# A decoder layer whose instructions are issued by a written list: another list, the same instructions

## The chip, the cores and the metric

The kernel runs on one core of one Trainium2 chip. The core has a matrix engine (PE, which reads its stationary operand through weight loads, PEld), a vector engine (DVE), a scalar engine (ACT), a GpSimd engine (POOL) and a queue for transfers (SP). Each works through its own instructions in the order in which they were issued, and waits for others through semaphores. The metric is the device time in microseconds (us) of one execution; several executions give a median.

## The reference, cut to what matters

One layer of a decoder on 256 positions and 1024 channels, all in float32. A recurrent branch and an attention branch with 8 heads of 128 read the same normalised input; their outputs are gated, merged and projected; a gated feed-forward part with a short convolution follows.

```python
h = rmsnorm(x, norm1_g[l])
u = jnp.einsum('bsd,de->bse', h, w_in[l])
x_rnn, g_rnn, q, k, v, g_br = jnp.split(u, list(cuts), axis=-1)
...
ya = rg_lru(xa, w_r[l], b_r[l], w_i[l], b_i[l], lru_lambda[l]) * jax.nn.gelu(g_rnn)
...
merged = (gates[:, :, 0] * jnp.einsum('bsc,cd->bsd', ya, w_proj_rnn[l])
          + gates[:, :, 1] * jnp.einsum('bsc,cd->bsd', yb, w_proj_attn[l]))
x = x + jnp.einsum('bsd,de->bse', merged, w_out[l])
h = rmsnorm(x, norm2_g[l])
up = causal_dwconv(jnp.einsum('bsd,df->bsf', h, w_up[l]), ffn_conv_w[l], ffn_conv_b[l])
act = jax.nn.gelu(up) * jnp.einsum('bsd,df->bsf', h, w_gate[l])
x = x + jnp.einsum('bsf,fd->bsd', act, w_down[l])
```

With 256 positions and a block of 256, the block-sparse attention is plain causal attention inside one block.

## The kernel before

**Weights and halves.** The weights come from memory in chunks of 1 MB, numbered in the order of use (4 and 5 are the first two of the recurrent input, 22 is the third of the gate "ga", 25 the last of "v"). A chunk is loaded into a buffer `raw` (three of them). ACT rounds it to a short form `hi` (four buffers) and DVE takes the rest `lo = raw - hi` (three buffers). Each product is then three matmuls: hi by hi, hi by lo, lo by hi. A `raw` buffer is free for the next load when its `lo` is done; a `hi` or `lo` buffer is free when PE has read it. Activations are split the same way (`xgh`, `xgl`; `qTh`, `qTl`; `kTh`, `kTl`; `pth`, `ptl`), mostly in 23 buffers of 1024 columns that go round.

**PE's order.** PE works through units of 24 matmuls of 512 columns per chunk: k0 to k3, rx0 to rx3, rg0 to rg3, ri0, q0, q1, ri1, ga0, ga1, q2, q3, v0, v1, ga2, ga3, v2, v3, gb0 to gb3, and so on, to the projections (pr, pa, wo), the feed-forward part (up, gt, and the blocks qA, qB, qC) and the down projection (acc). Small groups for the attention heads stand between: S of head h (six matmuls into tile `s`), and O (six into `o`). Head 3 comes first, then 2, 1, 0, then 4 to 7; S3 stands in v1, S2, S1 and S0 in ga2, S4 in v2, O3 and O0 in gb0 and gb1.

**The turn of q.** The units q2 and q3 leave the second half of q in two PSUM tiles, `q10` and `q11` (first and second 128 positions). Each tile has two readers: ACT squares it (`sqq`, for the norm), and DVE transposes its 32 by 32 blocks (`qd`). From `qd` the data go to memory and come back transposed (`qm`), and ACT and DVE split them into `qTh1` and `qTl1`, which S4 to S7 read.

**Issue.** The program first records every instruction without issuing it: 1130 of ACT, DVE, POOL and the queues, numbered 0 to 1129 as recorded, and 1899 of PE. Then `Later.issue` (lines 232 to 245) goes through the string `ORDER` (line 114 on): a number or a range issues those instructions, and `+n` the next n of PE.

```python
        for r in order.split():
            if r[0] == "+":
                ops += [next(pe) for _ in range(int(r))]
            else:
                ops += [self.ops[n] for n in range(int(r.split("-")[0]), int(r.split("-")[-1]) + 1)]
```

So PE's own order does not depend on the string. What the string sets is the order of each other engine's queue; which of the buffers a tile gets (`Pool.buffer` takes the one whose last use in the list is oldest); and what waits for what, where two instructions touch one tile. All instructions are issued from line 245, so every row of the profile has L245, and they are told apart by their tiles.

The numbers that matter below:

| number | engine | instruction |
|---|---|---|
| 161, 162, 163 | DVE | the first two scale k (`kr`), the third transposes it (`kd`) |
| 214, 286 | DVE | transpose the recurrent gate, `gr` from `gs` |
| 306, 308 / 309, 310 | DVE | sums of the squares of `q00`, `q01` / their transposes `qd` |
| 338, 341 | DVE | `lo` of chunks 18 and 19 (units q2 and q3) |
| 339 | SP | load of chunk 22 |
| 342, 343 | ACT, DVE | `qTh0`, `qTl0` |
| 344, 346 | ACT | squares `sqq` of `q10`, `q11` |
| 345, 347 | DVE | their sums |
| 348, 349 | DVE | transposes `qd` of `q10`, `q11` |
| 392, 393 | ACT, DVE | `hi`, `lo` of chunk 22 (unit ga2) |
| 411, 412 | ACT, DVE | `qTh1`, `qTl1` |
| 415 | DVE | a 128x2 product for the softmax of head 0 |
| 429 | DVE | `lo` of chunk 25 (unit v3) |
| 433 to 435 | ACT | tanh, exp, square for the second half of the recurrent gates (`tt1`, `rt1`, `a21`) |
| 515, 516 | ACT, DVE | `pth0`, `ptl0`, read by O0 |
| 586 to 589 | DVE | scans of the first half (`it0`) |
| 788 | SP | load of a 0.5 MB piece of the gate weight (`wq011`) |

Of the kernel before, what the change touches and what calls it, by code (L numbers as in the profile page):

```python
# [114 lines left out]
26 0 4 24-25 1 3 30 32 28 27 2 29 31 +2 5 +1 6 +1 7 +1 8 +1 9 +2 10 +1 11-13 +2 33-34 +3 35-36 15 +5 14 +2 37-38 +2
39-40 16 +5 41-42 18 +2 43-48 +2 17 +2 19 +3 49 51 50 52 23 +3 20 69 71 +6 55 72 21 +4 53 +2 59 57 +1 56 54 +4 60 22
+6 63 +3 58 +3 65-66 +1 64 61-62 +3 67-68 +19 76-77 +5 74-75 +2 96 105-106 +4 73 +1 99 +1 102 93 108 78-79 +15 104 +9
80 109 81-84 +11 107 +1 70 224-226 85-89 +1 90-91 +1 142-143 +7 110 +3 111-112 92 94 +3 95 187-188 +6 141 +5 114 113
+5 98 190 97 117-119 227-228 115-116 +5 186 +3 100 191 +2 204 +2 229 +7 203 +2 121 101 103 144 120 122 230 123 +1
# [15 lines left out]
511 +4 479 +1 513-514 501 515-516 485 512 488 502 486 503-504 559 +4 536-537 534 +2 535 +2 528 +5 477 +6 597 526 +6
539 560 +6 529 518 530 519 562 561 +1 547 +1 527 +2 563 +11 540-541 531-532 +2 525 +2 629 +8 574 +3 542 +3 549-550 +1
581 +2 551-552 +8 553 +1 557 +1 548 +11 564-566 568 618 +2 546 +1 594 +1 554 543 556 +1 544 +1 619 558 555 575 579
576-578 567 598 +7 620 545 +3 584 +6 569-571 601 +2 592 617 789 603 602 +5 595 +2 582 605 604 +6 596 +2 607 +2 580 +1
608 615 599 613 655 +12 606 +5 585 621 600 609-610 593 583 +13 616 +6 611-612 622-623 +18 627-628 +13 625-626 630 729
731 +4 730 +11 614 787 632 788 +5 640-641 +1 732 +8 634-635 +1 733-734 638 +4 790 +19 796 798 639 +1 624 644 785 +14  # L140
800 631 +6 646-647 +3 648-650 +6 636 633 663 637 +11 645 +4 654 653 652 651 +3 658 664 +1 786 670 +3 642 +1 656 659
643 +1 657 797 799 +15 662 661 +3 671 801 +11 669 +5 677 +6 660 665-666 +2 667-668 +4 697 +3 678 +9 672-673 +4 676 +6
674-675 +7 698 712 +10 696 +1 679-680 683 682 681 +12 695 702 +1 684-685 +3 713 +12 699 694 700-701 711 +12 716-717
+11 715 +10 686-687 +1 692 748 690 688 703 +2 704 725 724 +1 689 +1 691 706 705 708 710 707 709 714 961 751 765 727 +2
735 693 736-737 +2 738-741 +3 750 +9 742 728 743-745 960 +1 746-747 +5 766 +1 749 +10 726 997 +13 793 775-776 +6 791
+5 774 764 996 +9 719 718 720-722 +4 792 +6 998 +1 820 +1 723 752 755 758 +3 753 822 +1 784 +1 794 +2 759 +5 756 +2
803 802 +11 767 +3 821 823 +13 761-762 754 760 768-770 995 771 +11 826-827 +1 835 +4 773 772 +6 825 +1 795 757 +1
837-838 777 841 839 +3 994 +8 824 862 778 +1 804 +1 842 763 836 840 +13 779 782 999 783 +3 780-781 +3 828 +3 863 +1
866 864 +10 861 +2 877 808 816 875 829 +9 814 865 1005 867 +2 813 843 +3 845 +1 891 811 805 +1 878 1006 844 876 +11
812 810 807 +8 926 892 +10 817 +1 890 +1 806 868 1008 869-870 872-873 871 +10 927 +2 848 851 809 815 818 +7 855 854  # L150
849 852 929-930 846 879-880 +1 925 +4 1007 +11 874 955-956 +1 894 +7 819 893 +1 954 883 928 884 882 881 +17 964 958 +3
886-887 857 962 888-889 959 +2 847 858 856 +5 850 853 +3 957 +7 931 +3 932 +2 968 830 963 1009 833 859-860 +5 885 +20
969 965 1010 +3 1000 1002 +7 831 834 967 832 900 966 +2 917 +2 916 +8 1001 1011 1003 1012 +11 1018 1014-1015 +10 1016
918-919 +1 1013 +10 970 +4 1019 1017 1023 +8 971 +3 1024 993 1004 +1 1027 1025 +10 907 912 +1 1022 1021 +5 903 910 906
901 909 904 +6 905 +1 1028 1026 +1 1030 +8 911 908 +1 895-896 898-899 897 +2 1020 +4 1031 +2 1034 +7 902 913-914 +1
1029 +4 933 936 934 937 935 +6 1032-1033 +1 1039 +4 1035 +2 920 +6 1043 915 +2 1040 +11 1038 +3 938 +2 972 974-976 973
+5 1041-1042 +1 1053 +9 922 +2 1036 1078 1076 +1 921 1054 +10 1037 1044 1052 +3 923 +2 939-940 947 +7 950 944 977 +1
1077 +1 1088 +4 1079 +5 951 +2 1045 948-949 +1 1046 1050 1047 1049 1048 +3 941 +2 1091 +4 1089 945-946 952 +4 989 +6
982 987 986 +1 1055 924 +1 1087 +2 1056-1058 1061 1059 984 +5 1060 +5 1092 942-943 +2 1098 985 978 953 981 +5 1051 +1
1080 +7 988 979 1101 +3 1099 +1 1090 +7 1062 +3 1097 1081 1083-1085 1082 1086 +10 1093-1096 980 983 990-991 +2 1102 +8  # L160
1064 +5 1103 1063 1065-1067 +4 1068-1071 +7 1109 +5 1104 +3 1072-1075 +10 1110 +5 1100 +8 992 1106 1105 1107-1108 +5
1112-1113 +45 1111 +6 1114-1115 +5 1116-1117 +1 1118-1119 +3 1120-1121 +5 1122-1123 +3 1124-1125 +1 1126 +6 1128 1127
1129
"""


# [1174 lines left out]
```

## Time and profile before

| | |
|---|---|
| median of 3 executions | 428.87 us (427.77 to 428.91) |
| the profiled execution, its own time | 429.04 us |
| its span, first to last instruction | 427.3 us |
| matmuls | 1908, busy 418.9 us |
| DVE | 439, busy 359.5 us |
| ACT | 382, busy 305.7 us |
| POOL | 101, busy 52.3 us |
| read from memory | 92.63 MB |

The profile shows one execution. A row of the timeline gives the start, the duration, the engine, the operation and the tiles, and in square brackets the idle time of that engine ahead of it with what ended it. Durations of matmuls are modelled and overlap; what tells PE's pace is the step from one start to the next.

### The profile page before, as it was taken

To read this page: it belongs to the slowest core of one execution; us is meant where nothing else is said; L and a number is where in the kernel's file an instruction comes from. 1 tells how busy PE (TensorE), PEld (TensorE's weight loads), DVE (VectorE), ACT (ScalarE), POOL (GpSimd) and SP (SyncE) were. 2 spreads that over 40 slices of the span, in tenths; PEclk is the share of its full clock that TensorE was granted. 3 is DMA by queue.
4 is the path that set the end of the run, shared out by engine and by line. 5 is a ranking of instruction groups with operands and counts; after the bars stand their busy time and mean duration, and the time that the engine had idled before them with its cause. 6 is when DMAs were issued, how large, how long until landed. Compare 5 with 4: busy or idle time off the path is not lost.

```text
span 427.3 us, 5450 instructions
## 1 busy us (share of the span) xinstructions
PE 418.9 (98%) x1908; PEld 348.4 (82%) x1908; DVE 359.5 (84%) x439; ACT 305.7 (72%) x382; POOL 52.3 (12%) x101
## 2 busy tenths in 40 slices
...
GB/s 219 414 359 200 278 306 254 200 253 356 320 203 308 156 292 236 219 357 259 281 275 269 247 151 366 222 232 307 150 267 287 184 156 239 257 217 322 288 2 98
DMA packets 46108, 106.89 MB, mean 250 GB/s; under 512 B 8448, under 2 KB 22656, under 8 KB 43648
## 3 DMA queue, kind: packets, MB, share of 16 engines
...
q10 hardware_dynamic: 720, 0.53, 0.4%
...
q14 instruction: 13, 0.11, 0.1%
HBM read 92.63 MB, written 13.89 MB: 249 GB/s over the span
## 4 chain that ended last, share of the span: by engine, by line
PE 84%; DVE 7%; issue 3%; ACT 2%; DMA 1%; POOL 1%; SPq 0%; DVEq 0%; ACTq 0%
PE acc L245 14%; PE up L245 13%; PE k L245 5%; PE pr L245 5%; PE gb L245 5%; PE qA L245 5%; PE wo L245 5%; PE pa L245 5%; PE rg L245 5%; PE rx L245 5%; PE qC L245 3%; PE gt L245 3%; PE last L245 3%; PE v L245 2%; DVE lo L245 2%
## 5 line engine op out<-in xcount | busy, mean ns | idle before, releaser
L245 DVE TENSOR_TENSOR lo<-raw,hi 128x2048 fp32r<-128x2048 f32 (+1 forms) x64 | 141.7, 2217 | 19.3 <-ACT hi L245 16.1
L245 ACT CAST hi<-raw 128x2048 fp32r<-128x2048 f32 (+1 forms) x64 | 118.4, 1856 | 26.0 <-DMA raw<-in_wpa 6.8
L245 PE MATMUL up<-hi,h2l 128*128 128x512 f32 x80 | 31.1, 389 | 0.0
L245 PE MATMUL up<-hi,h2h 128*128 128x512 f32 x80 | 31.1, 389 | 0.0
L245 PE MATMUL up<-lo,h2h 128*128 128x512 f32 x80 | 31.1, 389 | 0.0
L245 PE MATMUL acc<-lo,fah 128*128 128x512 f32 x78 | 30.4, 390 | 0.0
L245 PE MATMUL acc<-hi,fah 128*128 128x512 f32 x78 | 30.4, 390 | 0.0
L245 PE MATMUL acc<-hi,fal 128*128 128x512 f32 x78 | 30.4, 389 | 0.0
L245 POOL TENSOR_TENSOR rsq<-rsq 128x8 f32<-128x8 f32 x32 | 21.0, 658 | 36.4 <-DVE rsq L245 34.3
L245 ACT ACT_TABLE_LOAD x15 | 19.2, 1283 | 1.4 <-PEq L1331 1.2
L245 PEld LDWEIGHTS up<-lo,h2h 128*128 128x128 f32 x80 | 15.0, 188 | 3.1
L245 PEld LDWEIGHTS up<-hi,h2l 128*128 128x128 f32 x80 | 15.0, 188 | 3.1
L245 PEld LDWEIGHTS up<-hi,h2h 128*128 128x128 f32 x80 | 15.0, 188 | 3.1
L245 PEld LDWEIGHTS acc<-hi,fal 128*128 128x128 f32 x78 | 14.6, 188 | 3.1
L245 PEld LDWEIGHTS acc<-hi,fah 128*128 128x128 f32 x78 | 14.6, 188 | 3.1
L245 PEld LDWEIGHTS acc<-lo,fah 128*128 128x128 f32 x78 | 14.6, 188 | 3.1
L245 DVE TENSOR_TENSOR loq<-wq,hiq 128x1024 fp32r<-128x1024 f32 x12 | 14.5, 1216 | 2.4 <-ACT fu L245 1.4
L245 DVE TENSOR_TENSOR lot<-wq,hit 128x1024 fp32r<-128x1024 f32 x12 | 14.4, 1219 | 2.2 <-PE last L245 1.6
L245 ACT ACTIVATE fu<-fupd,pv 128x256 f32<-128x256 f32 x32 | 14.7, 498 | 1.3 <-DVE fal L245 1.3
L245 DVE TENSOR_TENSOR wq<-wq,wq 128x1024 f32<-128x1024 f32 x12 | 14.5, 1219 | 0.2
L245 PE MATMUL ga<-lo,xgh 128*128 128x512 f32 x32 | 12.6, 394 | 1.8 <-DVE lo L245 1.8
L245 ACT CAST hit<-wq 128x1024 fp32r<-128x1024 f32 x12 | 12.3, 1049 | 2.6 <-DVE wq L245 1.7
(302 smaller groups left out, 1177.5 us busy)
## 6 DMA issues: line engine op xcount, KB each, us to landing
raw<-in_win_fm SPq DMA_DIRECT2D x16, 1024.0 KB, 7.3
raw<-in_wdown SPq DMA_DIRECT2D x11, 1024.0 KB, 6.1
raw<-in_wup SPq DMA_DIRECT2D x10, 1024.0 KB, 5.9
raw<-in_win_tm SPq DMA_DIRECT2D x8, 1024.0 KB, 6.0
...
raw<-in_wpr SPq DMA_DIRECT2D x4, 1024.0 KB, 5.8
raw<-in_wpa SPq DMA_DIRECT2D x4, 1024.0 KB, 6.3
...
```

The costliest lines, as they stand in the source:

```text
L245: getattr(engine, name)(*map(real, a), **{n: real(v) for n, v in k.items()})
```

## The change

Only the string `ORDER` differs. It names the same 1130 numbers and the same 1899 matmuls. Of the 423 instructions of DVE 219 stand at another place in DVE's queue, by at most 10 places; of ACT's 351 it is 205, by at most 12; of POOL's 97 it is 31, by at most 11; of the 259 transfers of SP it is 146, by at most 14. The largest shift on SP is 788, which goes ahead by 14. Its author states three rules by which the new list was searched: the readers of one PSUM tile run in the order in which they are issued; steps that depend on one another are chained; and GpSimd's waits are counted.

Cut to the stretch from unit q2 to unit v3 (chunks 18 to 25), with the lines that begin and end inside other stretches left whole:

```diff
-+1 241-242 +6 222 213 +2 211 223 +5 219 +4 282 +1 221 162 +1 243-246 +10 209 327 +1 193-194 271 263-265 275-278 +2 272
...
-303 330 +2 309 305-306 +3 307 +6 319-320 331 +6 321 +3 337 +3 324 +6 326 323 +1 308 362-363 329 +5 364-365 310 313-314
-311-312 +1 325 322 +2 430 338 +1 340 +8 318 +2 336 +5 341 431 440 +1 366-371 +9 328 339 +5 214 217 215 218 +5 441 334
-+1 372 +2 335 355 +2 373-375 443 286 356 +3 360-361 +7 289 354 287-288 442 432 +3 358 +8 376-378 +4 359 +2 216 +7 290
-+1 572-573 589 588 +2 357 +2 342-343 +3 291 +1 348 344-345 433 392 586 +3 349 351-353 350 346 393 +1 347 449 +6 450
-587 452 +3 451 453 +1 454-458 +11 422 434-435 +4 423 +1 391 +7 425 +2 292 402 421 +5 459-463 +7 380 379 381 +1 538 +2
-387 +3 389 +1 426 +11 394-395 436 388 390 +3 424 +5 382-385 +6 386 +2 428 404 +5 403 405-406 480 483 481 484 482 +5
-407 +2 437 396 411 398 +5 408-410 +5 413-416 397 417 +2 429 +8 447 +2 412 399 418 420 401 419 492 427 +1 444 +2 506
...
++3 179 198 180-181 222 +9 211 223 162 +9 282 +1 221 +1 244-247 +10
...
+165 167 317 +10 332-333 315 +5 166 164 +3 330 +2 309 305 +3 310 312 307 +6 319-320 331 308 306 +6 337 321-322 +12 326
+324-325 +1 362 286 363-364 366 329 +5 314 365 367-368 311 313 +3 214 430 338 +9 318 +2 336 +5 323 340-341 431 440-441
++1 369-372 +9 339 289 328 +5 216-217 215 290 218 288 +5 334 +3 335 +2 373-378 443 442 355-356 +3 360-361 432 +7 354
++15 358-359 +9 357 291 287 +1 572-573 589 +4 392 342-343 586 +4 344 433-435 +3 349 348 351 350 352 588 353 393 345-347
++1 449-450 +6 587 451 453 452 +3 454-455 +1 456 +11 422 +4 423 +1 391 +7 425 +2 402 292 421 +5 457-465 +7 379-380 +3
+387 +3 389 381-382 538 +1 426 +11 395 388 436 394 390 +3 424 +5 383-386 +4 403-404 +4 428 396 405 +5 480 482 484 481
+437 483 +5 407 406 408 410 409 +2 411 398 +10 413-414 412 415 397 416-417 +2 429 +8 447 +2 418 506 420 419 492 399 590
...
```

Sorted by engine, the places that the prediction speaks of are these (ranges shortened):

| queue | before | after |
|---|---|---|
| DVE, ahead of unit ga1 and q2 | `lo16`, `kTl0`, 163, 309, 306, `lo17`, 308, ..., 310, 430, 338, 341, 214, 443, 286 | 163, `lo16`, `kTl0`, 309, 310, `lo17`, 308, 306, ..., 286, ..., 214, 430, 338, 341, 443 |
| ACT, ahead of unit ga2 | 572, 342, 344, 433, 392, 346, 422, 434, 435 | 572, 392, 342, 344, 433, 434, 435, 346, 422 |
| DVE, ahead of unit ga2 | 573, 589, 588, 343, 348, 345, 586, 349, 393, 347 | 573, 589, 343, 586, 349, 348, 588, 393, 345, 347 |
| readers of `q10` in the list | 348 (DVE), then 344 (ACT) | 344 (ACT), then 348 (DVE) |
| DVE, ahead of S4 | 413, 414, 415, 429, 412 | 413, 414, 412, 415, 429 |
| SP, among the writes of heads 6 and 7 | 788 after the load of chunk 38 | 788 ahead of the four writes of head 7 |

More of the change, by code (lines that the diff above doesn't have):

```diff
@@ L114 @@
 ORDER = """
[L115 to L119, printed above, removed]
@@ L120 @@
-124-127 +3 145 +3 168 +1 170 205 +10 169 171 174-175 173 189 172 +1 128 +2 129-131 +1 132-133 231 207 +1 146 135 147
-+5 232 148 +4 208 134 136 +1 149-153 +9 177 +1 206 +1 176 199-201 195-196 182 +2 233-234 154 235 155-156 +4 140 192
-138 137 139 +1 157-158 236 159 +2 212 178 +1 183-185 +1 210 +4 220 +1 237-238 160 239-240 +3 197 179 198 202 180-181
-+1 241-242 +6 222 213 +2 211 223 +5 219 +4 282 +1 221 162 +1 243-246 +10 209 327 +1 193-194 271 263-265 275-278 +2 272
-+3 273 266 +1 247 +1 267-268 +1 248-249 +1 283 +7 294-295 285 +2 269 161 270 274 +2 250-254 +2 300 284 +6 302 301 +2
@@ L125 @@
-255-259 +11 297-298 +4 279-280 316 +2 281 +8 299 332 304 +2 296 260-262 +2 317 +10 333 163 315 +5 165 164 166-167 +3
-303 330 +2 309 305-306 +3 307 +6 319-320 331 +6 321 +3 337 +3 324 +6 326 323 +1 308 362-363 329 +5 364-365 310 313-314
-311-312 +1 325 322 +2 430 338 +1 340 +8 318 +2 336 +5 341 431 440 +1 366-371 +9 328 339 +5 214 217 215 218 +5 441 334
-+1 372 +2 335 355 +2 373-375 443 286 356 +3 360-361 +7 289 354 287-288 442 432 +3 358 +8 376-378 +4 359 +2 216 +7 290
-+1 572-573 589 588 +2 357 +2 342-343 +3 291 +1 348 344-345 433 392 586 +3 349 351-353 350 346 393 +1 347 449 +6 450
@@ L130 @@
-587 452 +3 451 453 +1 454-458 +11 422 434-435 +4 423 +1 391 +7 425 +2 292 402 421 +5 459-463 +7 380 379 381 +1 538 +2
-387 +3 389 +1 426 +11 394-395 436 388 390 +3 424 +5 382-385 +6 386 +2 428 404 +5 403 405-406 480 483 481 484 482 +5
-407 +2 437 396 411 398 +5 408-410 +5 413-416 397 417 +2 429 +8 447 +2 412 399 418 420 401 419 492 427 +1 444 +2 506
-508 510 489 496 494-495 507 493 +1 445 +2 475 +16 467 466 400 +2 464-465 590 468-469 438 +8 448 591 +3 476 520 +2 446
-+2 523 522 509 +2 521 524 505 +3 470-471 490-491 472-473 533 +1 478 +5 474 +1 517 +2 293 +5 498 439 487 497 499 +3 500
@@ L135 @@
[L135 to L163, printed above, removed]
+3 24 26 25 28 1 4 30 32 2 0 29 31 +2 5 33-34 +1 6 35 +1 7 37 +1 8 +1 9 +2 10 +1 11-13 +5 36 15 +5 14 +2 38 +2 39-40 16
++5 41-42 18 +2 43-48 +2 17 +2 19 +3 49-52 23 +3 71 20 27 69-70 224 +6 55 72 22 21 +4 53 +2 59 57 +1 56 54 +4 60 +6 63
@@ new lines @@
++3 58 +3 65-66 +1 64 61-62 +3 67-68 +19 76-77 +5 74-75 +2 105 108 96 106 +4 73 +1 99 +1 109 78 93 79-81 +15 104 +9
+82-86 +11 107 +1 225 87-91 142 92 +2 143 +7 110 95 97-98 +3 111-112 94 +3 187-188 +6 141 +5 113-114 +5 101-102 190
+117-120 226-228 121 229 116 115 +5 186 +3 191 100 +2 204 +2 122 +7 203 +2 103 144-146 123-124 +1 125-129 +6 168 +1 170
++10 169 171 205 175 189 174 173 172 +3 130-133 135 134 230-232 +1 207 +1 147 +5 233 148-149 +4 208 136 +1 150-151
+234-235 152-155 +9 177 +1 206 +1 176 199-201 195-196 182-183 +2 156-157 +4 137 192 139-140 138 +1 158-160 236-240 +2
@@ new lines @@
+210 178 +1 197 184 202 185 +2 213 +3 220 +1 241-243 +3 179 198 180-181 222 +9 211 223 162 +9 282 +1 221 +1 244-247 +10
+219 209 327 +1 193-194 263-266 212 267 275-276 +2 271-272 268 273 277-278 +6 248-253 +1 283 +1 285 +6 294 +2 269-270
+161 274 +2 254-255 +2 300 284 +6 302 295 299 297 301 +2 256-262 +4 303 +7 298 +4 279 304 280 316 +2 281 +10 296 +2 163
+165 167 317 +10 332-333 315 +5 166 164 +3 330 +2 309 305 +3 310 312 307 +6 319-320 331 308 306 +6 337 321-322 +12 326
+324-325 +1 362 286 363-364 366 329 +5 314 365 367-368 311 313 +3 214 430 338 +9 318 +2 336 +5 323 340-341 431 440-441
@@ new lines @@
+400-401 520 427 +1 444 +2 493-494 496 489 495 507-508 510 +1 445 +2 438 475 +16 466-467 +2 468-470 490 +8 448 +3 591
+476 +2 446 +2 505 522 509 +2 523-524 521 +3 439 491 487 471-473 533 +1 478 +5 474 +1 517 537 536 +7 497-499 +3 511 293
++3 501 515 513 +1 479 488 516 +1 500 514 502-503 512 485-486 504 +8 535 534 528 +5 477 +6 526 +3 529-530 597 +3
+559-560 539 +6 518-519 562 561 +2 527 +2 563 +11 540 547 541 531 +2 525 +2 629 +8 574 +6 549-550 532 551-552 +1 542
+581 +2 553 548 619 +9 557 544 +12 564-566 543 568 545 618 +2 546 +2 554 556 555 575 577-579 +2 598 558 576 567 569-570
@@ new lines @@
+620 594 +7 617 +3 584 +6 571 601 +2 592 788 603-604 789 605 602 +5 595 +2 582 +6 596 +2 607 +2 580 +1 608 655 599 615
++6 609 +6 606 +5 621 593 585 613 611 600 610 729 583 +13 616 +6 622-623 625 612 +18 627 +13 626 631 630 628 731-732 +4
+730 +11 787 614 632 790 785 +2 640-641 +12 634-635 +1 733 796 734 638 +23 798 639 +1 624 644 +14 800 +6 646 +3 648 647
+649-650 +6 636 633 637 +11 645 +4 651 654 653 652 +3 657 663-664 +1 786 670 +3 642 +1 656 659 643 +1 797 658 799 801
++15 661-662 +3 671 +11 669 +5 677 +6 660 665-666 +2 667-668 +4 697 +3 678 +9 672-673 +4 676 +6 674-675 +7 698 712 +10
@@ new lines @@
+696 +1 679-680 683 682 684 681 685 +12 695 702 +4 713 +12 699-700 694 701 711 +12 716-717 +11 715 +10 686-687 +1 688
+751 692 750 690 703 727 724 +2 704 725 765 +1 689 +1 706 705 691 710 707 709 708 997 714 961 +2 693 735-737 +2 738-742
++12 743-745 +1 728 746-747 +5 766 +11 774 726 +13 775 791 793 749 748 776 +11 998 764 960 +9 719 718 720-722 +4 792 +6
+996 +2 723 752-753 755 758 820 822 759 +4 784 +1 802 794 +9 754 803 761 +11 756 +3 768 821 823 760 +13 767 769 772
+770-771 995 +11 826-827 +5 773 +6 825 +1 795 757 +1 778 835 837 762-763 836 838 +3 994 +8 777 862 841 824 839 +1 804
@@ new lines @@
++1 842 840 +13 779 782 999 +3 781 780 783 845 +6 1005 863 +1 828 866 864 +10 861 +2 877 875 808 829 +9 867 865 +2 843
+813-814 807 891 811 816 805 +5 1006 876 878 844 +11 815 812 810 +8 926 892 +10 817 +1 890 +1 851 868 806 848 809 857
+1008 869 872 870-871 873 +10 927 +2 879 846 929-930 849 818 +7 855 854 852 955 819 880 1007 +1 925 +13 893 +2 874 830
+956 +1 962 964 +8 882 928 881 883-884 833 954 +17 958 +3 886-888 894 889 959 +2 847 853 850 858 856 +8 885 831 957 +7
+931 +5 968 963 965 859 1009 860 +25 969 1010 +10 832 834 966 900 967 +2 917 +2 916 +8 1002 1000 932 1003 1001 1011
@@ new lines @@
+1014 +11 1016 1018 1015 +10 918 +1 1013 +10 970 +3 971 +1 1012 1017 1019 919 1023 +11 1024 993 1004 +1 901 907 1025
++11 1022 1021 +5 909 912 904 1027 906 903 +6 905 +1 1026 1028 +1 910 1030 +9 895 899 898 896-897 +2 1020 +4 1031 +9
+1034 902 913 911 908 933 914 +1 1029 +4 935-936 934 937 +6 1032 1035 1033 +1 1039 +6 920 +6 915 1043 +2 1040 +11 1038
++3 938 +2 972-974 976 975 +5 1041 +1 1053 +9 921 +2 1036 922-923 1076 1078 +1 1054 1042 1044 +10 1037 1052 +5 940 939
+947 950 +7 977 +1 1077 +1 1088 944 +9 951 948 1079 949 +2 1045-1046 1048 1050 1049 +1 1047 +3 941 +2 1091 +4 1089
```

5 lines of the change are left out of this document (added).

## The prediction

> **What bounds the kernel now.** I read the page first.
>
> ```profile
> span 427.3 us, 5450 instructions
> ...
> PE 418.9 (98%) x1908; PEld 348.4 (82%) x1908; DVE 359.5 (84%) x439; ACT 305.7 (72%) x382; POOL 52.3 (12%) x101
> ```
>
> PE is busy for 98% of the span. A new order of the other queues cannot shorten PE's work; it can only take away what PE waits for. So the second view is PE's waits.
>
> ```profile
> PE s L245 <- DVE qTl L245: 2.3, 1, 2.3
> PE ga L245 <- DVE lo L245: 1.8, 1, 1.8
> ```
>
> The columns are total, count and longest. Past the start, PE waits only twice: the third matmul of S4 for `qTl1`, and the second of unit ga2 for `lo` of chunk 22. The third view is PE's timeline at both.
>
> ```profile
> 99.04 0.39 PE L245 MATMUL q<-hi,xgh 128*128 128x512 f32 x1
> 99.27 0.39 PE L245 MATMUL q<-lo,xgh 128*128 128x512 f32 x1
> ...
> 121.50 0.47 PE L245 MATMUL ga<-hi,xgh 128*128 128x512 f32 x1
> 123.80 0.50 PE L245 MATMUL ga<-lo,xgh 128*128 128x512 f32 x1 [1.83 <-DVE lo L245]
> ...
> 139.53 0.28 PE L245 MATMUL s<-kTl,qTh 128*128 128x128 f32 x1
> 142.14 0.33 PE L245 MATMUL s<-kTh,qTl 128*128 128x128 f32 x1 [2.34 <-DVE qTl L245]
> ...
> 143.18 0.39 PE L245 MATMUL v<-hi,xgl 128*128 128x512 f32 x1
> ...
> 144.09 0.63 PE L245 MATMUL v<-hi,xgl 128*128 128x512 f32 x1
> 144.52 0.63 PE L245 MATMUL v<-hi,xgh 128*128 128x512 f32 x1
> ...
> 147.05 0.40 PE L245 MATMUL v<-hi,xgh 128*128 128x512 f32 x1
> ```
>
> From start to start a matmul of 512 columns takes 0.23 us (99.04 to 99.27). The first stop costs 123.80 - 121.50 - 0.23 = 2.07 us. The second costs 142.14 - 139.53, less about 0.1 for a matmul of 128 columns, so 2.5 us. Behind it the step is 0.43 us (144.09 to 144.52): the ten steps from 143.18 to 147.05 take 3.87 us where ten of 0.227 would take 2.27. That is 1.6 us more, at half pace, and the windows below show a granted clock of 0.93 there and 1.00 around. The three terms are 2.07 + 2.5 + 1.6 = 6.17 us.
>
> **What the new order does to the first stop.** The next views are the timelines of ACT and DVE ahead of it.
>
> ```profile
> 116.56 0.69 ACT L245 ACTIVATE sqq<-q,rs 128x512 f32<-128x512 f32 x1 [6.04 <-DVE qd L245]
> 117.27 1.28 ACT L245 ACT_TABLE_LOAD   x1
> 118.56 1.06 ACT L245 ACTIVATE tt<-rt 128x1024 f32<-128x1024 f32 x1
> 119.53 1.89 ACT L245 CAST hi<-raw 128x2048 fp32r<-128x2048 f32 x1
> ...
> 136.60 1.05 ACT L245 ACTIVATE qTh<-qd 128x1024 fp32r<-128x1024 f32 x1
> ```
>
> ```profile
> 112.26 1.22 DVE L245 TENSOR_TENSOR it<-it,tt 128x1024 f32<-128x1024 f32 x1
> 113.51 1.27 DVE L245 TENSOR_TENSOR_SCAN it<-rt,it 128x256 f32<-128x256 f32 x2
> 114.70 1.20 DVE L245 TENSOR_TENSOR qTl<-qd,qTh 128x1024 fp32r<-128x1024 f32 x1
> 115.82 0.71 DVE L245 STREAM_TRANSPOSE qd<-q 128x512 f32<-128x512 f32 x1
> 117.28 0.69 DVE L245 TENSOR_REDUCE sq<-sqq 128x4 f32<-128x512 f32 x1 [0.76 <-ACT sqq L245]
> ...
> 121.45 2.29 DVE L245 TENSOR_TENSOR lo<-raw,hi 128x2048 fp32r<-128x2048 f32 x1 [2.28 <-ACT hi L245]
> ```
>
> ACT stands idle for 6.04 us until DVE has transposed `q10`, though the square does not read `qd`: both read one PSUM tile, and the second reader in the list waits for the first. Behind the square stand a table load (1.28), the tanh (1.06) and only then `hi` of chunk 22; DVE pauses 0.76 + 2.28 = 3.04 us. The new list puts 344 ahead of 348, and 392 ahead of 342, 344 and the tanh. So `hi` starts when the chunk is there.
>
> ```profile
> 100.23 0.49 SPq L245 DMA_DIRECT2D raw<-in_win_fm  x1
> ...
> raw<-in_win_fm SPq DMA_DIRECT2D x16, 1024.0 KB, 7.3
> ```
>
> Its load is issued at 100.23, or at most 2.5 us later if `lo19` slips (next part), and with the group's median of 7.3 us it lands by 110.0. Then `hi` ends at 111.9 and `qTh0` (1.05) at 113.0. DVE's new queue from 113.5 is a scan, `qTl0`, a scan, two transposes, a scan and `lo`: 0.6 + 1.2 + 0.6 + 0.7 + 0.7 + 0.6 + 2.29 = 6.7, so `lo` is done at 120.2. PE wants it at 121.50 + 0.23 = 121.73. The stop goes with 1.5 us to spare, and -2.07 us is the term. The moved transposes now wait for ACT's squares (`q10` at 113.7 at the latest), which come first here.
>
> **The second stop.**
>
> ```profile
> 138.66 2.29 DVE L245 TENSOR_TENSOR lo<-raw,hi 128x2048 fp32r<-128x2048 f32 x1
> 140.87 1.22 DVE L245 TENSOR_TENSOR qTl<-qd,qTh 128x1024 fp32r<-128x1024 f32 x1
> ```
>
> `qTl1` stood behind `lo` of chunk 25 (2.29) and a product of 0.16; now both are behind it. That is 2.45 us earlier, and the 3.04 us that DVE no longer pauses make it 140.87 - 5.49 = 135.4, done at 136.6. PE, 2.07 us ahead, is there at 142.14 - 2.5 - 2.07 = 137.6. One microsecond is to spare. It needs `qTh1` by 135.4, which now ends at 137.65: ACT must come 2.3 us earlier, and the pause that it loses is 6.04. The term is -2.5. `lo25`, which waits 1.2 us longer, is used a unit later.
>
> **The slow matmuls** go with the second stop: the slow pace is there within 2 us of it (142.14 to 144.09), and the first stop, shorter by 0.4 us, left none: the clock is 1.00 in the window around it. The term is -1.6. The Trainium skill (TensorE: Matmul & The Clock Gate, "What's actually happening") has the clock fall to half after at least one idle window of about 3.4 us, so by it a wait of 2.3 us would leave the clock alone. The measured half pace behind 2.34 us of waiting decides here; what the rule would leave is the first rival.
>
> **What the new order costs.** Each place below could give some back.
>
> ```profile
> 83.91 2.29 DVE L245 TENSOR_TENSOR lo<-raw,hi 128x2048 fp32r<-128x2048 f32 x1 [0.58 <-ACT hi L245]
> ...
> 89.90 0.69 DVE L245 TENSOR_REDUCE sq<-sqq 128x4 f32<-128x512 f32 x1 [0.76 <-ACT sqq L245]
> ...
> 95.72 2.28 DVE L245 TENSOR_TENSOR lo<-raw,hi 128x2048 fp32r<-128x2048 f32 x1
> ...
> 102.56 1.24 DVE L245 STREAM_TRANSPOSE gr<-gs 128x1024 f32<-128x1024 f32 x1
> ```
>
> Unit q2: two transposes of `gr`, 1.24 us each, now precede `lo18`, which ended at 98.00 and is wanted at 99.27. That is 2.48 against 1.27, so 1.2 us late. But 163 moves into the pause of 0.58 us, and 310 into that of 0.76: 1.34 us come back, and 0.1 is to spare. Bounds 0 and 1.2; I take 0, since those pauses end on ACT and both moved instructions have their data.
>
> Units v3 to gb3: PE is 6.17 us ahead of its old times; the others must follow.
>
> ```profile
> 119.00:142.00 23.00, 18.98 (x95) 15.63 (x93) 20.11 (x43) 22.24 (x31) 7.42 (x13) 1.00 0.62 217
> 142.00:165.00 23.00, 22.86 (x104) 19.20 (x105) 21.76 (x45) 22.47 (x30) 0.00 (x0) 0.93 0.84 265
> 165.00:183.00 18.00, 18.00 (x96) 15.39 (x95) 17.09 (x31) 17.93 (x26) 0.00 (x0) 1.00 0.70 221
> ```
>
> ```profile
> 159.25 0.56 DVE L245 TENSOR_TENSOR ptl<-pd,pth 128x384 fp32r<-128x384 f32 x1 [0.23 <-ACT pth L245]
> ...
> 162.19 0.28 PE L245 MATMUL o<-ptl,vh 128*128 128x256 f32 x1
> ...
> 192.70 2.29 DVE L245 TENSOR_TENSOR lo<-raw,hi 128x2048 fp32r<-128x2048 f32 x1 [2.16 <-PE pr L245]
> ...
> 204.13 0.39 PE L245 MATMUL pa<-lo,ybh 128*128 128x512 f32 x1
> ```
>
> The busy columns are PE, PEld, DVE, ACT and POOL. DVE (20.11 of 23, 21.76 of 23, 17.09 of 18) and ACT (22.24, 22.47, 17.93) have hardly a pause, so they come forward by what they no longer wait: 3.04 us and up to 6.04. The tightest product is `ptl0`, done at 159.81 and wanted at 162.19: 2.38 to spare. With DVE 3.04 earlier that covers 5.42 of 6.17, so PE could wait 0.75 us at O0; if nothing came forward, 3.8. The writes and the read of `pd0` are issued earlier in the new list. Between 0 and 3.8 I take 0.3, half of the DVE figure, and count it in the forecast. Where the other engines wait for PE itself, they come forward with it.
>
> The queues: 788, moved ahead on SP by 14 transfers, brings 0.5 MB, 2.4 us at the 221 GB/s of that window, ahead of head 7's writes and the load of chunk 34. `lo34` ends at 194.99 and is used at 204.13; 9.1 - 6.2 - 2.4 is still positive, so 0. The buffer that it fills was last read by S7, which PE has then passed, so SP does not stop there. POOL's moved steps interleave two chains that both end before a waiting DVE step; I take 0, with the 0.3 as its bound.
>
> **The sum.** The profiled execution took 429.04 us, 1.74 outside its span. 429.04 - 6.17 + 0.3 = 423.17; the median lies 0.17 under it. The forecast is **423.0 us**, 1.4% faster.
>
> **The rivals.**
> - *The slow pace stays.* If its cause were not the stop (the rule named above), only 4.57 us go: 428.87 - 4.57 = 424.3. For it: a shorter stop left the pace alone. Against: the clock is under 1.00 only in the window that begins with that stop.
> - *Given back at the heads.* DVE and ACT, full, do not follow; O0 waits up to 3.8 us, over 2.3, and half pace follows with 1.6: 423.0 - 0.3 + 5.4 = 428.1 at worst; at 2 us, without the slow pace, 424.7. With the 1.2 us of q2, 425.9.
> - *The stops stay.* If the reader that waits is set by something else than the list, ACT keeps its 6.04 us, `qTh1` holds S4, and little changes: 428.5.
> - *Slower: chunk 22 lands late.* In the new ACT queue `hi22` blocks `qTh0` and the square, and so DVE's `qTl0` and transposes. From the end of `hi22`, `qTh0`, `qTl0`, two scans, two transposes and `lo22` take 1.05 + 1.2 + 1.2 + 1.4 + 2.29 = 7.1 us, so PE stops from a landing at 121.73 - 7.1 - 1.89 = 112.7 on. A landing X later costs X + 1.6 at ga2 and X - 1 + 1.6 at S4. Above X = 2, that is a landing over 12 us after issue, it costs more than 5.9; at X = 4 it is 428.87 - 6.17 + 10.2 = 432.9. The median landing of 7.3 speaks against it.
>
> **How the numbers follow.** Forecast 0.57; slow pace stays 0.05; given back 0.20; stops stay 0.08; slower 0.10. A change of 0.3% (1.3 us) is about the least that a measurement of this kernel tells from none. Faster by more than that is under 427.6: forecast, slow pace and nearly all of "given back", 0.80. Within: the stops that stay and the rest of that, 0.11. Slower: 0.09. The range runs from 422.0 (no wait at O0, and 0.7 of spread) to 427.4 (nearly the worst of "given back") and leaves out the last two cases.
>
> **What would show it.** Right: PE's waits hold neither `ga <- lo` nor `s <- qTl`; no step of 0.43 us after the start; a granted clock of 1.00 throughout; ACT's 6.04 us in front of `sqq` gone; `lo22` ends by 120.5 and `qTl1` by 137. Wrong: a new wait of PE on `q <- lo`, `o <- ptl`, `wo <- ml` or `acc <- fal`, above all one over 2 us with slow steps behind it.

## The result, and the profile after

The changed list takes **423.19 us** in the median of 4 executions (422.61 to 423.42) against 428.74 for the list before (4 executions, 427.77 to 428.91). The ratio is 0.9873, with a 95% interval from 0.9855 to 0.9891: 1.3% faster. The forecast was 423.0. The profiled execution took 422.61 us; that of the kernel before took 429.04, so between the two profiles lie 6.43 us.

The first page lines of the changed kernel, span, busy time and the chain that ended last (its rows have L243, since the string is two lines shorter):

```profile
span 420.8 us, 5449 instructions
...
PE 416.6 (99%) x1908; PEld 347.2 (83%) x1908; DVE 358.5 (85%) x439; ACT 307.5 (73%) x382; POOL 51.1 (12%) x101
...
PE 99%; DVE 0%; issue 0%
```

The busy times of DVE, ACT and POOL are within 2 us of what they were. The chain that ended last is PE almost alone (99%). PE's waits, all of them:

```profile
PE warm L243 <- DVE ones L243: 1.0, 1, 1.0
```

That one is the start. Both rows of before, `ga <- lo` and `s <- qTl`, are gone. PE's timeline at the two places, and at O0, where a new wait was feared:

```profile
121.76 0.39 PE L243 MATMUL ga<-lo,xgh 128*128 128x512 f32 x1
...
137.47 0.27 PE L243 MATMUL s<-kTh,qTl 128*128 128x128 f32 x1
...
155.88 0.28 PE L243 MATMUL o<-ptl,vh 128*128 128x256 f32 x1
```

The first two are the matmuls that waited in the kernel before, the third is the one feared for. The second of ga2 starts at 121.76 instead of 123.80, 2.04 us earlier; the third of S4 at 137.47 instead of 142.14, 4.67 earlier; the second of O0 at 155.88 instead of 162.19, 6.31 earlier. So the gain comes in three steps of 2.04, 2.63 and 1.64 us, and PE keeps it to the end. The windows of the same two stretches as before:

```profile
119.00:142.00 23.00, 23.00 (x117) 19.52 (x116) 22.23 (x52) 20.79 (x31) 7.53 (x13) 1.00 0.75 250
142.00:165.00 23.00, 23.00 (x121) 19.64 (x120) 21.78 (x42) 22.63 (x31) 0.00 (x0) 1.00 0.85 259
```

The columns are those of before: PE is busy for all of both stretches, and the granted clock, third from the end, is 1.00 in both (0.93 in the second before). What made it possible, on ACT and on DVE:

```profile
107.86 1.90 ACT L243 CAST hi<-raw 128x2048 fp32r<-128x2048 f32 x1
...
110.61 0.67 ACT L243 ACTIVATE sqq<-q,rs 128x512 f32<-128x512 f32 x1
```

```profile
114.27 2.26 DVE L243 TENSOR_TENSOR lo<-raw,hi 128x2048 fp32r<-128x2048 f32 x1
...
131.98 1.22 DVE L243 TENSOR_TENSOR qTl<-qd,qTh 128x1024 fp32r<-128x1024 f32 x1
...
151.93 0.56 DVE L243 TENSOR_TENSOR ptl<-pd,pth 128x384 fp32r<-128x384 f32 x1 [0.28 <-ACT pth L243]
```

The square has no bracket now: the 6.04 us ahead of it are gone. `lo22` ends at 114.27 + 2.26 = 116.5 and is read at 121.76; `qTl1` ends at 133.2 and is read at 137.47; `ptl0` ends at 152.5 and is read at 155.88. So PE finds them ready with 5.2, 4.3 and 3.4 us to spare, far more than was worked out (1.5, 1.0 and -0.75).

### The profile page after: what moved, and what is told of

Same layout as the page of the kernel before. It is cut to its first block, busy times and chain, and to the rows that moved or that the text cites. A ratio compares the mean times of both kernels' runs of the same rounds, so it can differ in the third digit from the quotient of the medians.

```text
span 420.8 us, 5449 instructions
## 1 busy us (share of the span) xinstructions
PE 416.6 (99%) x1908; PEld 347.2 (83%) x1908; DVE 358.5 (85%) x439; ACT 307.5 (73%) x382; POOL 51.1 (12%) x101
## 4 chain that ended last, share of the span: by engine, by line
PE 99%; DVE 0%; issue 0%
PE acc L243 14%; PE up L243 13%; PE k L243 5%; PE gb L243 5%; PE pr L243 5%; PE qA L243 5%; PE wo L243 5%; PE ga L243 5%; PE v L243 5%; PE q L243 5%; PE pa L243 5%; PE rg L243 5%; PE rx L243 5%; PE qC L243 3%; PE last L243 3%; PE gt L243 3%
## 5 line engine op out<-in xcount | busy, mean ns | idle before, releaser
L243 DVE TENSOR_TENSOR lo<-raw,hi 128x2048 fp32r<-128x2048 f32 (+1 forms) x64 | 141.7, 2216 | 14.8 <-ACT hi L243 9.4
L243 ACT CAST hi<-raw 128x2048 fp32r<-128x2048 f32 (+1 forms) x64 | 118.7, 1860 | 26.8 <-DMA raw<-in_wpa 7.1
L243 PE MATMUL up<-hi,h2l 128*128 128x512 f32 x80 | 31.1, 389 | 0.0
L243 PE MATMUL up<-hi,h2h 128*128 128x512 f32 x80 | 31.1, 389 | 0.0
L243 PE MATMUL up<-lo,h2h 128*128 128x512 f32 x80 | 31.1, 389 | 0.0
L243 PE MATMUL acc<-lo,fah 128*128 128x512 f32 x78 | 30.4, 389 | 0.0
L243 PE MATMUL acc<-hi,fah 128*128 128x512 f32 x78 | 30.4, 389 | 0.0
L243 PE MATMUL acc<-hi,fal 128*128 128x512 f32 x78 | 30.3, 389 | 0.0
L243 POOL TENSOR_TENSOR rsq<-rsq 128x8 f32<-128x8 f32 x32 | 18.7, 585 | 29.5 <-DVE rsq L243 27.5
L243 DVE TENSOR_TENSOR loq<-wq,hiq 128x1024 fp32r<-128x1024 f32 x12 | 14.4, 1220 | 4.0 <-PE up L243 3.2
L243 PEld LDWEIGHTS up<-hi,h2l 128*128 128x128 f32 x80 | 15.0, 188 | 3.1
L243 PEld LDWEIGHTS up<-hi,h2h 128*128 128x128 f32 x80 | 15.0, 188 | 3.1
L243 PEld LDWEIGHTS up<-lo,h2h 128*128 128x128 f32 x80 | 15.0, 188 | 3.1
L243 PEld LDWEIGHTS acc<-hi,fah 128*128 128x128 f32 x78 | 14.6, 188 | 3.1
L243 PEld LDWEIGHTS acc<-lo,fah 128*128 128x128 f32 x78 | 14.6, 188 | 3.0
L243 PEld LDWEIGHTS acc<-hi,fal 128*128 128x128 f32 x78 | 14.6, 188 | 3.0
L243 DVE TENSOR_TENSOR lot<-wq,hit 128x1024 fp32r<-128x1024 f32 x12 | 14.1, 1221 | 2.4 <-PE acc L243 1.8
L243 ACT CAST hiq<-wq 128x1024 fp32r<-128x1024 f32 x12 | 12.1, 1051 | 4.3 <-PE up L243 3.5
L243 ACT ACTIVATE fu<-fupd,pv 128x256 f32<-128x256 f32 x32 | 14.6, 510 | 0.7 <-DVE fal L243 0.7
L243 DVE TENSOR_TENSOR wq<-wq,wq 128x1024 f32<-128x1024 f32 x12 | 14.6, 1218 | 0.1
L243 POOL TENSOR_SCALAR decw<-decw 128x8 f32<-128x8 f32 x17 | 11.1, 652 | 20.4 <-ACT decw L243 19.1
```

Of the source, the lines that this page charges most:

```text
L243: getattr(engine, name)(*map(real, a), **{n: real(v) for n, v in k.items()})
```

## The experiments

Three questions were put. Which part of the long diff carries the gain? Are the two moves that the prediction named enough, or needed? And is the half pace behind S4 the price of the stop? The diffs show the places of the string at which a kernel differs from the list named.

**The early part alone, the late part alone.** The string was divided at the 294th matmul (unit ri0, 70.6 us). `early_only` has the new list up to there and the old one behind; `late_only` the reverse.

> The new list up to unit ri0 (PE time 70.6 us), the old list from there. Theory E (the early part matters: GpSimd's chain for the norm of k ends 5 us earlier there, and DVE's wait of 2.3 us for it at 57 us is gone): DVE and ACT run about 2.3 us ahead from 70 us on; in the old order behind, lo of chunk 22 then ends at about 121.4 against 121.7 wanted, so the first stop is gone or under 0.3 us; qTl1 ends at 139.8 at the latest against 137.6 wanted, so a second stop of 1 to 2.2 us stays. Time 423.5 to 426.0. Theory L (only the moves next to the stops matter): both stops stay as they were, 428.7 within 0.5.

> The old list up to unit ri0, the new list from there. Theory L, as the prediction worked it out: both stops gone, lo of chunk 22 done by 119 and qTl1 by 136.6, slow pace gone, 422.7 to 423.2. Theory E: without the early part DVE has 2.3 us less to spare; a wait of up to 1.2 us comes back at unit q2 (lo of chunk 18), or a small one at S4, 423.5 to 425.

`early_only`: 426.23 us (424.72 to 427.57, 10 executions), ratio 0.9958 (0.994 to 0.9976). `late_only`: 422.84 us (422.29 to 422.89, 4), ratio 0.9882 (0.9862 to 0.9902), which cannot be told from the full change. The late part alone is enough for the whole gain; the early part alone brings a third of it (0.4%), which is not added to it when both are there. PE's waits in `late_only`, and what is left at S4 in `early_only`:

```profile
PE warm L244 <- DVE ones L244: 1.0, 1, 1.0
PE k L244 <- ACT his L244: 0.2, 1, 0.2
```

```profile
137.31 0.28 PE L245 MATMUL s<-kTl,qTh 128*128 128x128 f32 x1
139.50 0.33 PE L245 MATMUL s<-kTh,qTl 128*128 128x128 f32 x1 [1.92 <-DVE qTl L245]
```

The early part does bring DVE forward, by 2.6 us at `lo22` and `qTl1`, most of it the 2.3 us that DVE waited for `rk` at 57 us, and that removes the first stop by itself: `lo22` ends at 121.1 in `early_only`, PE needs it at 121.72. But it leaves a second stop of 2.1 us (139.50 - 137.31, less 0.1), with steps of 0.43 us behind it in this profile. The median lies 0.2 us above the expected range, in which the half pace was not counted. Where the late part is there too, the early part buys only reserve: in `late_only` `lo22` starts at 116.31 and `qTl1` at 133.82, 2.0 and 1.8 us later than in the full change, and still done 3.3 and 2.6 us before PE needs them.

**One move: the square ahead of the transpose** (`reader_only`, the list before with this):

```diff
-+1 348 344-345 433
++1 344 348 345 433
```

> The old list with one number moved: the square 344 of q10 ahead of the transpose 348 of the same PSUM tile. If the list alone decides which reader waits: ACT's pause of 6.0 us ahead of the square goes, hi of chunk 22 ends at 115.4, DVE no longer pauses and lo ends at 120.7 (wanted 121.7): the first stop gone; DVE comes 3.0 us forward, so qTl1 ends at 139.1 against 137.6 wanted: a second stop of 1.5 us instead of 2.5. With the slow pace gone (it needs a longer stop) 424.0, with the slow pace staying 425.6. If something else sets the reader that waits: 428.7, unchanged, with ACT's pause still there.

424.43 us (424.22 to 424.97, 4), ratio 0.9924 (0.9904 to 0.9944): a single swap, alone, is worth about 60% of what the whole change is worth. The ACT timeline shows the chain that the prediction named:

```profile
110.70 0.66 ACT L245 ACTIVATE sqq<-q,rs 128x512 f32<-128x512 f32 x1
111.38 1.28 ACT L245 ACT_TABLE_LOAD   x1
112.67 1.06 ACT L245 ACTIVATE tt<-rt 128x1024 f32<-128x1024 f32 x1
113.64 1.90 ACT L245 CAST hi<-raw 128x2048 fp32r<-128x2048 f32 x1
118.16 0.69 ACT L245 ACTIVATE sqq<-q,rs 128x512 f32<-128x512 f32 x1 [2.62 <-DVE qd L245]
```

The square starts 5.86 us earlier than before (116.56), and `hi22` 5.89 earlier (119.53). The 2.62 us at the end are the same wait again, for the other tile: 346 still stands behind 349. So the list decides which of two readers of one PSUM tile waits. PE's timeline at S4:

```profile
137.17 0.28 PE L245 MATMUL s<-kTl,qTh 128*128 128x128 f32 x1
138.98 0.33 PE L245 MATMUL s<-kTh,qTl 128*128 128x128 f32 x1 [1.53 <-DVE qTl L245]
```

The second stop is 1.7 us (1.81 less 0.1) instead of 2.5, since DVE came forward by more than PE did; no step of 0.43 us follows it.

**The other cure of the first stop** (`hi22_ahead`, the list before with `hi22` ahead of `qTh0`, the square left where it was):

```diff
-+2 342-343 ... 433 392 586
++2 392 342-343 ... 433 586
```

> The old list with one move: 392 (hi of chunk 22) ahead of 342, so also ahead of the square 344, which still waits for DVE's transpose 348. Theory (the first stop has two causes in series: the square that waits 6.04 us, and hi of chunk 22 that stands behind it): hi22 starts when its chunk is there and ends by 112, lo of chunk 22 no longer pauses 2.28 us for it, and the first stop is 0 to 0.3 us instead of 2.07. The square still waits for the transpose, so ACT and DVE come forward by less than in reader_only, qTl1 still stands behind lo of chunk 25, and S4 stops for 2 to 4 us because PE arrives 2 us sooner. Time 424.5 to 426.5 us, the spread being the half pace behind that stop. Rival (the reader order alone carries the first stop): hi22 early only moves the wait, ga2 still stops for about 2 us and the time stays at 427.5 to 428.9.

426.98 us (425.41 to 428.25, 10), ratio 0.9967 (0.9946 to 0.9989); the median lies 0.5 above the expected range. The ACT timeline:

```profile
109.69 1.92 ACT L245 CAST hi<-raw 128x2048 fp32r<-128x2048 f32 x1
...
116.68 0.69 ACT L245 ACTIVATE sqq<-q,rs 128x512 f32<-128x512 f32 x1 [4.11 <-DVE qd L245]
```

and PE at S4, where the matmul before started at 137.59:

```profile
140.46 0.47 PE L245 MATMUL s<-kTh,qTl 128*128 128x128 f32 x1 [2.60 <-DVE qTl L245]
```

The square starts as late as before, and yet the first stop is gone: `lo22` ran from 119.22 and ended 0.5 us ahead of PE. So the two moves are two cures of one stop. But here ACT keeps its wait, `qTl1` came forward by only 1.7 us (139.19) and PE by 1.9, and the stop at S4 stays: 2.8 us (140.46 - 137.59, less 0.1).

**Two moves** (`three_moves`, which in spite of its name has two: the swap of `reader_only`, and `qTl1` ahead of `lo25`):

```diff
-+1 348 344-345 433 ... +5 413-416 397 ... +2 412 399
++1 344 348 345 433 ... +5 413-414 412 415-416 397 ... +2 399
```

> The old list with two numbers moved: 344 ahead of 348, and qTl1 (412) ahead of 415 and of lo of chunk 25 (429). If the two stops are all that the new list takes away: both gone, lo of chunk 22 at 120.7, qTl1 at 136.6 against 137.6 wanted, 422.7 to 423.2, the time of the whole new list. If the other 600 moved places carry a share of the gain, it stays above 424.

424.61 us (423.81 to 426.42, 6), ratio 0.9929 (0.9908 to 0.995). Not what was expected: both stops are gone, the half pace too, and the time is that of `reader_only`. PE's timeline at O0 has what took it back:

```profile
155.75 0.39 PE L245 MATMUL gb<-hi,xgl 128*128 128x512 f32 x1
156.90 0.39 PE L245 MATMUL o<-pth,vh 128*128 128x256 f32 x1 [0.76 <-ACT pth L245]
157.49 0.39 PE L245 MATMUL o<-ptl,vh 128*128 128x256 f32 x1 [0.21 <-DVE ptl L245]
```

156.90 - 155.75 - 0.23 and 157.49 - 156.90 - 0.11 make 1.4 us. In this list ACT rounds `pth0` at 156.34, behind two exponentials and two copies of v; in the full new list it does so at 151.40, behind one exponential. The rival "given back at the heads" is real, and the rest of the new list is what prevents it. One of the six executions (426.42) has a granted clock of 0.996, which the profiled one does not show.

**`pth0` as well** (`pth0_too`: the two moves, and 515 and 516 moved ahead by a few places):

```diff
-+3 500 ... +1 513-514 501 515-516 485
++3 515 500 ... +1 513 516 514 501 485
```

> The run with two moves (344 ahead of 348, qTl1 ahead of lo of chunk 25) has no stop at ga2 and S4, but PE waits at O0, because ACT comes to pth0 (515) at 156.3 only, behind two exps and two copies of v. This kernel adds two moves: 515 ahead of 500, 516 ahead of 514. If ACT's order is what gives 1.4 us back at O0: pth0 starts when the read of pd0 has landed, about 154.6, ptl0 ends at 155.7, PE wants them at 155.7 and 155.9, so the wait at O0 is under 0.3 us and the time 423.0 to 423.5. If the transfer of pd0 is what is late (its writes and its read are issued 6 us later than in the new list): pth0 stays at 156 and the time near 424.5.

424.79 us (423.53 to 427.4, 10), ratio 0.9925 (0.9901 to 0.9949), so no faster than `three_moves`, and above both expected times. In the profiled execution (423.75 us) the wait at O0 is gone and PE reads `pth0` at 155.87, within 0.11 us of the full list. ACT rounds `pth0` at 153.02 there, so the transfer of `pd0` was not what was late. PE's waits show one further on:

```profile
PE warm L245 <- DVE ones L245: 1.0, 1, 1.0
PE pr L245 <- DVE yal L245: 0.4, 1, 0.4
```

The matmul that waits starts 0.78 us behind the one before it (180.45 to 181.23) instead of 0.23, a loss of 0.55. That profile supports a wait that moves on. The median of all ten lies another microsecond up, and what those executions lose was not seen; two of them (426.87 and 427.40) have a granted clock of 0.995.

**The full list without the two moves** (`undo_both`: the new list with 348 ahead of 344 and 412 behind 429 again):

```diff
-+4 344 ... 349 348 351 ... +10 413-414 412 415 397 ... 429 +8
++4 348 344 ... 349 351 ... +10 413-415 397 ... 429 412 +8
```

> The new list with both moves taken back: 348 ahead of 344 again, and lo of chunk 25 ahead of qTl1. If each of the two moves carries its own term of the prediction, the stops return: 425 to 429. If the new list holds more than is needed (its qTl1 ends 4.3 us before PE wants it, lo of chunk 22 5.2 us before): ACT's square starts about 3 us later than in the new list and qTl1 ends 2.3 to 4.5 us later, at 135.5 to 137.7 against 137.5, so at most 0.3 us of waiting: 422.7 to 423.7.

423.23 us (422.63 to 423.31, 4), ratio 0.9884 (0.9855 to 0.9913): as fast as the full change. PE's timeline at S4 and DVE's ahead of it:

```profile
137.88 0.28 PE L244 MATMUL s<-kTl,qTh 128*128 128x128 f32 x1
137.99 0.27 PE L244 MATMUL s<-kTh,qTl 128*128 128x128 f32 x1
```

```profile
134.25 2.29 DVE L244 TENSOR_TENSOR lo<-raw,hi 128x2048 fp32r<-128x2048 f32 x1
136.46 1.22 DVE L244 TENSOR_TENSOR qTl<-qd,qTh 128x1024 fp32r<-128x1024 f32 x1
```

`qTl1` ends at 137.68, 0.3 us ahead of PE. Neither move is needed once everything else stands as in the new list: `hi22` is ahead of the square there, so that the square's wait for the transpose, which is back (2.81 us), does not hold it up; and the rest brings DVE forward by 4.4 us (140.87 to 136.46).

**The stop put back.** The new list issues `qTl1` five or seven times more in a row (the diff shows seven; the line that asserts the number of instructions is left out):

```diff
-413-414 412
+413-414 412 412 412 412 412 412 412 412
```

> The new list, with qTl1 (412) computed five times more ahead of itself; its value does not change. Each costs DVE 1.15 us, 4.3 us are to spare, so PE stops at S4 for about 1.4 us. If the slow pace needs an idle time of a whole window of about 3.4 us, or one close to the 2.5 us of the old list, no step of 0.43 us follows: 424.2 to 424.8, all executions alike. If any stop of over a microsecond brings it: 425.8 to 426.4.

> The new list, with qTl1 computed seven times more: PE stops at S4 for about 3.7 us. If the length of the stop brings the slow pace, it follows in every execution: 422.9 + 3.7 + 1.6 = 428.2, within 0.5. If the slow pace of the old list came from something other than the stop: 426.6.

`late_by_5`: 425.8 us (425.39 to 426.71, 8), ratio 0.9951 (0.9935 to 0.9967). `late_by_7`: 429.88 us (428.46 to 430.37, 8), ratio 1.0035 (1.0015 to 1.0055). PE's timeline of `late_by_5`, then that of `late_by_7`, where the stop begins at 137.47:

```profile
137.68 0.28 PE L243 MATMUL s<-kTl,qTh 128*128 128x128 f32 x1
139.88 0.33 PE L243 MATMUL s<-kTh,qTl 128*128 128x128 f32 x1 [1.93 <-DVE qTl L243]
...
140.92 0.39 PE L243 MATMUL v<-hi,xgl 128*128 128x512 f32 x1
141.15 0.40 PE L243 MATMUL v<-hi,xgh 128*128 128x512 f32 x1
```

```profile
142.20 0.48 PE L243 MATMUL s<-kTh,qTl 128*128 128x128 f32 x1 [4.45 <-DVE qTl L243]
...
143.22 0.63 PE L243 MATMUL v<-hi,xgh 128*128 128x512 f32 x1
143.65 0.63 PE L243 MATMUL v<-lo,xgh 128*128 128x512 f32 x1
```

Both stops are longer than was expected (2.1 us, which is 139.88 - 137.68 less 0.1, for 1.4; 4.6, which is 4.73 less 0.1, for 3.7). The stop of 2.1 us left the pace at 0.23. So `late_by_5` fell into the range that was expected with the half pace (425.8 to 426.4) without it: the longer stop makes 2.1 of its 2.6 us. The stop of 4.6 us halved the pace at once. The two further copies made the stop 2.5 us longer and the kernel 4.1 us slower (425.8 to 429.88); the 1.6 us above the stop are about what the nine steps of 0.43 us in its profile cost over nine of 0.227, 1.8 us.

**The kernel before, three times more** (unchanged; `before_again_1` to `_3`).

> The kernel before, unchanged, for a second profile. Theory A (the 2.5 us stop at S4 brings the half pace in some executions only): the stop at ga2 is 2.0 to 2.1 and that at S4 2.4 to 2.6 us again; the time is near 427.2 where no steps of 0.43 us follow, and near 428.8 where they do. Theory B (the same stop always brings them, and the two groups of times differ in something else): ten steps of 0.43 us in this profile too, whatever its time.

> As before_again_1, a third profile. Theory A: of the three profiles of this kernel at least one has no steps of 0.43 us and takes about 1.6 us less than one that has them. Theory B: all have them.

> The kernel before once more. Its executions with a granted clock of 0.995 or 0.996 lie in two groups, 426.96 to 427.84 and 428.18 to 429.82. If this one falls in the lower group, theory A (only the start differs from execution to execution) has the first matmul of ga2 1 to 1.6 us earlier than the 121.50 of the first profile, with both stops and the slow pace unchanged; theory B (the stops differ) has it at 121.5 and the stops or the slow pace shorter by that much. If it falls in the upper group it only adds a fourth profile with stops of 2.0 to 2.1 and 2.4 to 2.6 us.

429.84, 427.5 and 427.75 us. The timeline of PE around S4 and the window of that stretch, in `before_again_2`:

```profile
139.61 0.28 PE L245 MATMUL s<-kTl,qTh 128*128 128x128 f32 x1
142.22 0.33 PE L245 MATMUL s<-kTh,qTl 128*128 128x128 f32 x1 [2.33 <-DVE qTl L245]
...
144.20 0.39 PE L245 MATMUL v<-hi,xgh 128*128 128x512 f32 x1
144.43 0.40 PE L245 MATMUL v<-lo,xgh 128*128 128x512 f32 x1
```

```profile
142.00:165.00 23.00, 22.78 (x114) 19.37 (x115) 21.77 (x45) 22.49 (x30) 0.00 (x0) 1.00 0.84 264
```

The same of `before_again_1`:

```profile
140.01 0.28 PE L245 MATMUL s<-kTl,qTh 128*128 128x128 f32 x1
142.62 0.33 PE L245 MATMUL s<-kTh,qTl 128*128 128x128 f32 x1 [2.34 <-DVE qTl L245]
...
144.01 0.63 PE L245 MATMUL v<-hi,xgh 128*128 128x512 f32 x1
144.44 0.63 PE L245 MATMUL v<-lo,xgh 128*128 128x512 f32 x1
```

```profile
142.00:165.00 23.00, 22.38 (x102) 18.77 (x103) 21.77 (x45) 22.48 (x29) 0.00 (x0) 0.93 0.82 262
```

The same stop to 0.01 us, once with the half pace behind it and once without. `before_again_3` has the stop (2.61 from start to start) and no slow step either. So the stop brings the half pace in some executions only. `before_again_3` was to tell why the times of this kernel that come with a clock of 0.995 or 0.996 lie in two groups. Its clock was 1.00, so that stays open.

## Why the prediction was right, and where its steps were not

**The three terms.** The forecast was 423.0 us, the median is 423.19. The terms 2.07, 2.5 and 1.6 us, together 6.17, measured 2.04, 2.63 and 1.64, together 6.31 at O0 and 6.43 in the profiled times. That the stops, and not PE's work, were what a new order could take away is shown by the waits after. That the median agrees to 0.2 us is in part luck: the profiled execution (422.61) is 0.56 us faster than the sum for it (423.17), because the 0.3 us at O0 did not occur and the terms are 0.26 larger; and the median lies 0.58 above that execution, not 0.17 under it.

**The first stop.** The chain transpose, square, table load, tanh, `hi22` is shown by `reader_only`. The prediction told the reader order and the early `hi22` as one cure; they are two, and each is enough (`reader_only`, `hi22_ahead`). The early part of the list is a third (`early_only`).

**The second stop.** `qTl1` ahead of `lo25` was counted as its cure. It is one (`three_moves` has no wait there), but `undo_both` shows that in the full list it is not needed. The prediction's term was right, its cause too narrow: of the 8.9 us by which `qTl1` came earlier (140.87 to 131.98), 2.45 are the swap and the rest is DVE's lead; 4.4 us come without either move (`undo_both`).

**The step that failed: how far DVE and ACT come forward.** The prediction let DVE gain 3.04 us, the two pauses at chunk 22, and put the moved steps of POOL at 0. DVE's wait for POOL at 57 us stood in the profile of before and was not weighed. POOL's timeline in the kernel before, then DVE's:

```profile
51.33 2.25 POOL L245 TENSOR_TENSOR rsq<-rsq 128x8 f32<-128x8 f32 x1 [4.03 <-DVE rsq L245]
53.54 0.20 POOL L245 TENSOR_TENSOR decw<-decw 128x8 f32<-128x8 f32 x1
```

```profile
51.23 2.29 DVE L245 TENSOR_TENSOR lo<-raw,hi 128x2048 fp32r<-128x2048 f32 x1
...
56.99 0.69 DVE L245 TENSOR_TENSOR kr<-kr,rk 128x512 f32<-128x512 f32 x1 [2.27 <-POOL rk L245]
```

The POOL operation of 53.54, of the same kind and size, took 0.20 us; that of 51.33 took 2.25, and ended at 53.58, with DVE's subtraction (53.52). At 57.71 another one takes 2.32 us, beside DVE's next subtraction (57.69 to 59.97). The Trainium skill (SBUF — State Buffer, "Who interferes with whom") says that a DVE instruction with two SBUF inputs contends with a GpSimd instruction that reads SBUF, and that the shared pair of ports is an exclusive lock; these rows agree. Without the 2.05 us that POOL lost there, DVE's pause would, by these rows, have been some 0.2 us. In the new list POOL's chain runs while DVE is not subtracting, and ends at 51.9, 5.1 us earlier than before (56.96):

```profile
51.39 0.21 POOL L243 TENSOR_TENSOR rk<-rsq 128x8 f32<-128x8 f32 x1
51.68 0.20 POOL L243 TENSOR_TENSOR rk<-rk,rs 128x8 f32<-128x8 f32 x1
```

At most 2.05 of these 5.1 us can be the blocked operation. The larger part is the 4.03 us in the brackets above: POOL waited for a small step of DVE (`rsq`, at 51.02), which stood behind another subtraction (47.52 to 49.80) in the old list. In the new one DVE does the three small steps for this norm together (45.05), ahead of its next subtraction (45.52). No run moved these steps alone; `early_only` moves them with the rest of the early part, and has no wait for `rk`. So DVE's pause of 2.27 us falls away, and DVE is ahead from 55 us on (`kr` at 54.59 instead of 56.99). At q2 `lo18`, given 0.1 us to spare, had 3.4 (done at 95.9, wanted at 99.30); in `late_only`, which still has the pause (2.24 us), it had 0.6 (98.8, wanted at 99.44).

A second part was in the prediction's own rows: the pauses of 0.58 and 0.76 us ahead of q2, into which 163 and 310 move, were counted at q2 and not behind it. In `late_only`, where both are gone, the scan that was taken to start at 113.5 starts at 112.20. With these 1.3 us, and the 2.0 and 1.8 of the early part, the 1.5 and 1.0 us to spare at the two stops become 4.8 and 4.1; measured were 5.2 and 4.3. The step made the forecast's reserves too small, not its time wrong: `late_only` is as fast without the early part's 2 us.

**The 0.3 us at O0** did not occur. It was bounded by letting `ptl0` come forward with DVE's 3.04 us; it came 7.3 us forward (159.25 to 151.93), and 5.6 in `late_only`, where PE still had 1.8 us to spare at O0. That the danger was rightly placed is shown by `three_moves`, which pays 1.4 us there.

**The slow matmuls.** The term of 1.6 us is right for the profile that it was read from, and taking the stop away takes it away. But it was told as a fixed price of the stop, and the runs say that it comes in some executions only: two of four profiles of the kernel before have it. Of the 55 executions that stood beside the experiments as reference, 47 show a granted clock of 0.995 or 0.996, with a mean of 428.28 us, and 8 show 1.00, with a mean of 427.50. Between these means lie 0.8 us, half of the profile's term. The 47 are the two groups named above: 20 of them, 426.96 to 427.84, are no slower than those at 1.00, and 27, 428.18 to 429.82, lie 1.4 us above those at 1.00 in the mean. In `hi22_ahead` the means are 427.4 (7 executions) and 425.7 (3), 1.7 apart. The forecast did not hang on this term: `before_again_2`, which has no slow step, took 427.50 us, and less its two stops of 1.9 (121.73 to 123.89, less 0.23) and 2.5 us that is 423.1. A profile of the kernel before without the half pace would have led to the same time after, as a smaller gain.

**The rivals.** "The slow pace stays", "given back at the heads", "the stops stay" and "chunk 22 lands late" did not happen in the full list; the second did in `three_moves`. Against the first stands that all four executions have a clock of 0.999 or 1.00; against the last, that the load of chunk 22 was issued at 98.15 and `hi22` began at 107.86 with no wait ahead of it.
